# Five big, thirteen middle and fourteen small expert places instead of six big and twenty-six middle

## The chip, the cores and the metric

One core of one Trainium2 chip runs the whole program. The metric is the device time of one execution in microseconds, the median of several runs. A profiled execution gives the trace: each engine's instructions, the DMA transfers and the granted clock of TensorE.

## The reference

The program computes three transformer layers for one sequence of 256 tokens of 1024 channels. The first layer has a differential and a neighbourhood attention and then a mixture of experts; the other two are a retention and sparse-attention mixer, a gated recurrence, and two dense feed-forward layers. The change is in the mixture of experts alone, which in the reference comes down to this:

```python
logits = (hf @ w_router + b_router).astype(jnp.float32)     # 256 tokens, 32 experts
top_val, top_idx = lax.top_k(logits, TOP_K)                 # TOP_K = 4
gates = jax.nn.softmax(top_val, axis=-1)
...
hh = xb @ w1[e] + b1[e]                                     # 1024 -> 2048
return swiglu_clamped(hh) @ w2[e] + b2[e]                   # 1024 -> 1024
...
out = jnp.einsum('tk,tkd->td', gates.astype(y.dtype), y)
```

`swiglu_clamped` takes the even columns of `hh` as gate and the odd ones as line. Each token goes to four of the 32 experts, so an expert has 32 tokens on the mean, and some have many more. All weights are float32: an expert has 8 MB of `w1` and 4 MB of `w2`.

## The kernel before

The experts are worked off in 32 places, in a loop over `p` in `experts()` (L890). A place has a fixed number of slots for tokens, in units of `CAP` = 64: `UNITS` gives two units (128 slots) to places 0, 5, 10, 15, 20 and 25 and one unit (64 slots) to the other 26. Expert 0 has place 0, because its weights can be loaded before the routing is known. The other experts are sorted by their number of tokens on the chip (`places()`, L621), and the largest get the big places, through a table of ranks (`order` in `prep`). A token beyond the slots of its place would be computed by `overflow()` (L1032), a branch over all experts that is taken only if there is such a token.

The weights of a place come as 12 tiles of [128, 2048] float32 (1 MB): eight of `w1`, one for each chunk `dc` of 128 input channels, and four of `w2`. `load_e` (L782) issues them on SP's queue into a ring of 13 slots, always in the order of their use (`tile_e`, L771); a load waits until the products of the tile that has its slot are done. Loads and products are in the order in which the code writes them, since TensorE and SP are scheduled by hand in this stage.

For a place of 64 slots the tokens are the stationary operand, [128, 64], and the weights stream through in pieces of 512 columns. Two products, for two pieces of columns, go to partitions 0 to 63 and 64 to 127 of the output, as two column tiles of the array. A float32 product shows in the trace as two instructions, so a tile of `w1` is eight instructions (`w1`, L914; all products are recorded at L89 by the helper `mm`). For a place of 128 slots the full width of the array is taken, and every half tile of weights is first split in two exact parts by ScalarE and VectorE (`split_e`, L789), for three products in a faster format (`product`, L1023).

Column tiles of 32 occur in the kernel already: `ada_rows` and `steps_ada` multiply a vector with `w_ada` at the start of the program, four pieces of 512 columns at once on four groups of 32 partitions (tiles `ps_s<-w,cs` in the trace; the prediction calls them the adaptive rows).

One turn of the loop over `p` goes: evacuate the first products of `p` (`evac`, L797, its two ScalarE copies are recorded at L803); the first `w1` tile of place `p + 1`; transposes and activation of `p` (`swiglu`, L806); two more `w1` tiles of `p + 1`; the one-hot of the slots (`one_hot`, L832); the four `w2` tiles of `p`; the other five `w1` tiles of `p + 1`, with steps between them that scatter the rows of `p` to their tokens (`scatter`, L849) or gather the tokens of a later group of places (`gather`, L723). A group takes consecutive places up to four units; a gather is four products of each half of the tokens with a one-hot of up to 256 columns.

After the last place, `first_ffn` (L871) loads eight tiles of the next layer on the same queue (L62), adds the gated sum to the residual, and the mixer of the second block begins.

Of the kernel before, what the change touches and what calls it, by code (L numbers as in the profile page):

```python
# [21 lines left out]
UNITS = [2 if p in (0, 5, 10, 15, 20, 25) else 1 for p in range(NE)]  # L22
# [7 lines left out]
class Block:  # L30
# [34 lines left out]
    def prepare(self, src, pool, tags, w=None, lo_on=None):  # L65
        """takes the next product's first weight tile and splits it ahead of the products."""
        nc = self.nc
        w = w or self.load_w(src, 2048)
        parts = [pool.tile([128, 2, 1024], F32R, name=t) for t in tags]
        for q in range(2):  # L70
            wq = w[:, q * 1024:q * 1024 + 1024]
            hi, lo = (t[:, q] for t in parts)
            nc.scalar.copy(hi, wq)
            (lo_on or nc.vector).tensor_tensor(lo, wq, hi.bitcast(F32), op=OP.subtract)
            self.halves.append((hi, lo))
        self.ahead.insert(0, w)
# [88 lines left out]
    def spread(self):  # L165
        """1 / rms by token along the free axis, on every partition."""
# [34 lines left out]
    def proj_tm(self, src, hh, hl, n=512):  # L201
        """token-major product of a [128, 8, n] weight group: psum [128, 2, n]."""
# [5 lines left out]
    def steps_tm(self, p, src, hh, hl, n=512):  # L208
        """the same in four steps."""
# [14 lines left out]
    def proj_out(self, src, nk, mh, ml, by=1):  # L224
        """token-major product of nk [128, 1024] weight rows: two psum tiles [128, 2, 512], as in down()."""
# [29 lines left out]
    def softmax_unit(self, P, s, bias, rs):  # L255
        """P = exp(s + bias - max), row sums in rs."""
# [50 lines left out]
    def steps_ada(self, p, c0, n):  # L307
        """a step for each weight tile."""
# [11 lines left out]
    def ada_cols(self, rows):  # L320
        """[128, quadrant, 4] columns of the four pieces."""
# [5 lines left out]
    def gate_parts(self, rows, prow):  # L327
        """(gate + bias) * g_post in the rows, still in their parts."""
# [3 lines left out]
    def gate_rows(self, dst, rows):  # L332
        """dst [128, 1024] = the rows on every partition."""
# [195 lines left out]
    def transpose_probs(self, P):  # L529
        """P [128 q, 2 qt, 256 k] -> [128 k, 2 kc, 256 q] in sbuf."""  # L530
# [9 lines left out]
    def add_gated(self, srcs, g):  # L540
        """x += g * rms(src)"""
# [12 lines left out]

    def route(self):
        """the four experts of a token, their gates and the places of the tokens in the experts."""
# [54 lines left out]
        # experts by their number of tokens; expert 0 keeps the first place  # L611
# [9 lines left out]
    def places(self):  # L621
        """experts in the order of their places, and what belongs to them."""
# [54 lines left out]
    def biases(self):  # L677
        """the first biases at the places of their experts, [128 f, gate or line, (f block, half), place]; two steps."""
# [20 lines left out]
    def late(self):  # L699
        """steps: the second biases, and whether a token is beyond its expert's slots."""  # L700
# [22 lines left out]
    def gather(self, ps):  # L723
        """transposed, modulated tokens of the places ps, [128, 8, slots] each, and the steps that make them."""
        nc = self.nc
        n = sum(UNITS[p] for p in ps) * CAP
# [7 lines left out]
        for p in ps:  # L734
            w = UNITS[p] * CAP
            at[p] = slice(k, k + w)
            k += w
            if UNITS[p] == 2:
# [7 lines left out]
        def onehot():  # L746
            for p in ps:
                for tt in range(2):
                    self.last_oh = nc.vector.tensor_scalar(oh[:, tt, at[p]], self.slots[:, CAP:CAP + UNITS[p] * CAP],
# [21 lines left out]
    def tile_e(self):  # L771
        """the place of the weight tile that comes next for the products."""
# [16 lines left out]
    def split_e(self, w):  # L789
        """a half of a weight tile in two exact parts."""  # L790
# [6 lines left out]
    def evac(self, hid, hs, late):  # L797
        """products [128, 2, 512], even and odd columns apart."""
        copy = self.nc.vector.tensor_copy if late else self.nc.scalar.copy
        hp = hid.rearrange("p a (j two) -> p two a j", two=2)  # L800
# [5 lines left out]
    def swiglu(self, hs, b1):  # L806
        """act [128 f, blocks of f, slots]; b1 [128, 2, blocks]."""
        nc, moe = self.nc, self.moe
        k = b1.shape[2]
        pg, pu = self.bank("s"), self.bank("s")  # L810
        for j in range(4):
            nc.tensor.transpose(pg[:, j * 128:j * 128 + 128], hs[:, 0, j * 128:j * 128 + 128], self.ident)
        for j in range(4):
            nc.tensor.transpose(pu[:, j * 128:j * 128 + 128], hs[:, 1, j * 128:j * 128 + 128], self.ident)
        view = lambda t: t.rearrange("p (j s) -> p j s", j=k)

        def biased(ps, u, name):
            t = moe.tile([128, 512], F32, name=name)
            nc.vector.tensor_tensor(view(t), view(ps), b1[:, u, :, None].to_broadcast([128, k, 512 // k]), op=OP.add)
            return t  # L820
# [3 lines left out]
        act = moe.tile([128, 512], F32, name="act", bufs=2)  # L824
# [7 lines left out]
    def one_hot(self, p):  # L832
        """tokens of the slots [slot, token], and the gates of the slots."""
        nc, moe = self.nc, self.moe
        s = self.slots[:, 64:192] if UNITS[p] == 2 else self.slots[:, 0:128]
        wt = self.bank("t")
        for tt in range(2):
            go = moe.tile([128, 128], F32, name="go", bufs=2)
            nc.vector.tensor_scalar(go, s, self.pos[:, tt, p:p + 1], self.G[:, tt, p:p + 1], op0=OP.is_equal,
# [9 lines left out]
    def scatter(self, ys, ot, gs, first):  # L849
        """steps that add the gated rows to their tokens; ys: one [(half, slot), 512], or two halves [slot, 512]."""  # L850
# [39 lines left out]
    def experts(self):  # L890
# [3 lines left out]
        for p in range(1, NE):  # L894
            if len(groups) <= 2 or sum(UNITS[q] for q in groups[-1]) + UNITS[p] > 4:
                groups.append([])
# [17 lines left out]
        def w1(p, dc, w=None):  # L914
# [5 lines left out]
            if p not in hids:  # L920
                hids[p] = [self.acc() for _ in range(UNITS[p])]
            w = w or self.load_e("w1", ids[p], dc)
            for m in range(2):
                if UNITS[p] == 2:
                    self.product(hids[p][m], Xs[p][0][:, dc], Xs[p][1][:, dc], w[:, m * 1024:m * 1024 + 1024], dc)
            if UNITS[p] == 1:
# [45 lines left out]
        for p in range(NE):  # L972
            hs = self.ap.tile([128, 2, 2, 512], F32, name="hs", tag="hh")
            hs = [self.evac(h, hs[:, m], m) for m, h in enumerate(hids[p])]
# [5 lines left out]
            two = UNITS[p] == 2  # L980
            b1 = self.b1[:, :, :, p]
            acts = [self.swiglu(h, b1[:, :, m::2] if two else b1) for m, h in enumerate(hs)]
# [11 lines left out]
            for c2 in range(4):  # L994
                w = self.load_e("w2", ids[p], c2) if p else w20[c2]
                for j in range(2):
                    c = 2 * c2 + j
                    wj = w[:, j * 1024:j * 1024 + 1024]
                    if two:
                        k = slice((c % 4) * 128, (c % 4) * 128 + 128)  # L1000
                        self.product(ys, parts[c // 4][0][:, k], parts[c // 4][1][:, k], wj, c)
                    else:
# [20 lines left out]
    def product(self, outs, xh, xl, w, k):  # L1023
        """outs [128 slots] += x @ half a weight tile, in three exact products."""
# [7 lines left out]
    def overflow(self):  # L1032
        """the tokens beyond the slots: every expert over all tokens, gated by what is left."""
# [56 lines left out]

    def even_mixer(self):
# [16 lines left out]
        # compressed keys and values  # L1108
# [140 lines left out]
        # retention  # L1249
# [64 lines left out]
    def odd_mixer(self):  # L1314
# [19 lines left out]
        for h in range(8):  # L1334
# [36 lines left out]
            while L <= 128:  # L1371
# [16 lines left out]
                # the second blocks of qp and the first of ks, T - L further on  # L1388
# [97 lines left out]
    def finish(self, ys):  # L1486
        """rms(x + ys) * final_g; ys: a psum tile for each half of the tokens."""
# [66 lines left out]
def prep(i, cap=CAP):  # L1554
    """Lays the inputs out; the tables depend on shapes alone."""
# [34 lines left out]
    c0[:, 672:704] = np.array(UNITS) * cap  # L1590
    order = [p for p in range(1, NE) if UNITS[p] == 2] + [p for p in range(1, NE) if UNITS[p] == 1]
# [106 lines left out]
```

## Time and profile before

| What | us |
|---|---|
| median of 3 runs (lowest, highest) | 1940.81 (1940.6, 1941.16) |
| the profiled execution: first to last instruction (its span; no other time of it is listed) | 1948.8 |
| TensorE busy in it | 1863.1 (96%) |
| VectorE, ScalarE busy | 1029.9 (53%), 728.9 (37%) |
| weights of the experts: 384 loads of 1024 KB, first and last issue | 142.3, 1206.5 |

The times of the trace count from the first instruction of the profiled execution. A matmul's end is modelled and overlaps the start of the next, so a busy TensorE may still be waiting for the next operand; the starts are the surer reading. A load has an issue time, on SP's queue, and a landing.

### The profile page before, as it was taken

The numbers are of one execution on the slowest core, as the hardware profiler recorded it, in microseconds if no ns is written. First come the engines' busy times: TensorE is split into PE (matmuls) and PEld (weight loads), VectorE is DVE, ScalarE is ACT, GpSimd is POOL, SyncE is SP. The second block draws the span as 40 slices with busy tenths as digits, with TensorE's granted clock in tenths as the row PEclk, the third lists the DMA queues.
The fourth block names the chain that finished last, engine by engine and source line by source line (L and its number), as shares of the span: only waits on it lengthen the run. The fifth ranks groups of instructions, "written<-read, shape, count | busy, mean of one in ns | idle before, by whom it ended". The sixth has DMA issues, their size and how long they took to land. (4 is left out here: it accounts for less than half of the span.)

```text
span 1948.8 us, 27834 instructions
## 1 busy us (share of the span) xinstructions
PE 1863.1 (96%) x10815; PEld 1195.1 (61%) x10815; DVE 1029.9 (53%) x1795; ACT 728.9 (37%) x1250; POOL 53.1 (3%) x101
## 2 busy tenths in 40 slices
PE   6999999999999999989999999799999999999998
PEld 4776653454353354445345433487899988779997
DVE  3555653463463265346347232457666666856555
ACT  3445531342251142234134101345544444545443
POOL 0000000000000000000000000200000000110000
PEclk8999899999999999999999999899999999999999
DMA  9874689999989999998999999642455544344540
GB/s 395 308 257 191 264 337 422 420 352 385 422 344 403 421 398 370 392 420 323 416 421 357 390 415 421 241 152 87 152 196 193 190 171 140 118 154 169 180 170 22
DMA packets 79992, 564.28 MB, mean 290 GB/s; under 512 B 8960, under 2 KB 9120, under 8 KB 13296
## 3 DMA queue, kind: packets, MB, share of 16 engines
q1 hardware_dynamic: 78800, 557.58, 72.7%
q0 software_dynamic: 1056, 4.87, 0.7%
q8 instruction: 87, 1.43, 0.3%
q14 instruction: 49, 0.40, 0.1%
HBM read 561.37 MB, written 1.05 MB: 289 GB/s over the span
## 5 line engine op out<-in xcount | busy, mean ns | idle before, releaser
L89 PE MATMUL acc<-w,X 128*64 128x512 f32 x1664 | 392.0, 601 | 0.2 <-ACT hs L803 0.2
L85 DVE TENSOR_TENSOR wlo<-w,whi 128x1024 fp32r<-128x1024 f32 (+1 forms) x232 | 281.0, 1214 | 185.0 <-ACT whi L84 184.7
L84 ACT CAST whi<-w 128x1024 fp32r<-128x1024 f32 (+1 forms) x232 | 240.9, 1044 | 315.6 <-PE acc L89 131.4
L89 PEld LDWEIGHTS acc<-w,X 128*64 128x64 f32 x1664 | 106.7, 136 | 203.7 <-issue 187.6
L794 DVE TENSOR_TENSOR elo<-w,ehi 128x1024 fp32r<-128x1024 f32 x144 | 174.5, 1221 | 35.1 <-ACT ehi L793 34.4
L89 PE MATMUL ps_s<-w,act 128*64 128x512 f32 x832 | 185.6, 599 | 3.0 <-issue 3.0
L793 ACT CAST ehi<-w 128x1024 fp32r<-128x1024 f32 x144 | 149.6, 1049 | 69.8 <-PE acc L89 52.4
L867 DVE TENSOR_TENSOR macc<-macc,ps_t 128x512 f32<-128x512 f32 x124 | 84.2, 687 | 142.8 <-PE ps_t L89 142.8
L856 DVE SCALAR_TENSOR_TENSOR yl<-ps_s,gslot,yh 128x512 fp32r<-128x512 f32 x38 | 28.0, 749 | 193.1 <-ACT yh L855 193.1
L89 PEld LDWEIGHTS ps_s<-w,act 128*64 128x64 f32 x832 | 58.0, 138 | 112.1 <-issue 103.1
L803 ACT COPY hs<-acc 128x512 f32<-128x512 f32 x64 | 34.4, 589 | 222.7 <-PE acc L89 222.7
L89 PE MATMUL acc<-hh,whi 128*128 128x256 f32 x368 | 109.5, 298 | 2.0 <-ACT whi L84 2.0
L89 PE MATMUL acc<-hl,whi 128*128 128x256 f32 x368 | 107.0, 291 | 0.0
L89 PE MATMUL acc<-hh,wlo 128*128 128x256 f32 x368 | 106.4, 289 | 0.5 <-DVE wlo L85 0.5
L89 PE MATMUL ps_s<-hh,whi 128*128 128x256 f32 x352 | 98.7, 280 | 0.0
L89 PE MATMUL ps_s<-hl,whi 128*128 128x256 f32 x352 | 98.3, 279 | 0.0
L89 PE MATMUL ps_s<-hh,wlo 128*128 128x256 f32 x352 | 98.2, 279 | 0.0
L855 ACT ACTIVATE yh<-ps_s,gslot 128x512 fp32r<-128x512 f32 x38 | 25.5, 687 | 187.0 <-PE ps_s L89 187.0
L89 PE MATMUL ps_t<-hh,whi 128*128 128x256 f32 x320 | 89.4, 279 | 0.0
L89 PE MATMUL ps_t<-hl,whi 128*128 128x256 f32 x320 | 89.3, 279 | 0.0
L89 PE MATMUL ps_t<-hh,wlo 128*128 128x256 f32 x320 | 89.3, 279 | 0.0
L89 PE MATMUL acc<-ehi,Xh 128*128 128x512 f32 x192 | 67.5, 434 | 14.5 <-ACT ehi L793 13.1
(423 smaller groups left out, 3383.5 us busy)
## 6 DMA issues: line engine op xcount, KB each, us to landing
w<-in_w_dram SPq DMA_DIRECT2D x384, 1024.0 KB, 9.9
w<-in_ffn_dram SPq DMA_DIRECT2D x66, 1024.0 KB, 4.7
w<-in_w_ada_dram SPq DMA_DIRECT2D x24, 1024.0 KB, 10.6
w<-in_w_in_dram SPq DMA_DIRECT2D x12, 1024.0 KB, 11.5
w<-in_even_cm_dram SPq DMA_DIRECT2D x8, 1024.0 KB, 7.0
w<-in_odd_qf_dram SPq DMA_DIRECT2D x8, 1024.0 KB, 5.3
w<-in_w_out_dram SPq DMA_DIRECT2D x4, 1024.0 KB, 8.2
w<-in_even_tm_dram SPq DMA_DIRECT2D x4, 1024.0 KB, 5.2
```

Source lines behind the costliest of these rows:

```text
L84: nc.scalar.copy(hi[:, :n], w)
L85: nc.vector.tensor_tensor(lo[:, :n], w, hi[:, :n].bitcast(F32), op=OP.subtract)
L89: self.nc.tensor.matmul(out, lhsT, rhs, start=start, stop=stop, skip_group_check=True)
L793: self.nc.scalar.copy(hi, w)
L794: self.nc.vector.tensor_tensor(lo, w, hi.bitcast(F32), op=OP.subtract)
L803: copy(hv[:, u], hp[:, u])
L855: nc.scalar.activation(yh[:, m], y, AF.Copy, scale=gs)
L856: nc.vector.scalar_tensor_tensor(yl[:, m], y, gs, yh[:, m].bitcast(F32), op0=OP.mult, op1=OP.subtract)
L867: nc.vector.tensor_tensor(self.macc[:, tt, m], self.macc[:, tt, m], q, op=OP.add)
```

## The change

A third class of place has 32 slots. Big places (128 slots) are 0, 4, 9, 14 and 19; places of 64 slots are 13 others; the remaining 14, among them 1, 5, 8, 10, 15, 20 and 24 to 31, have 32. The number of slots of each place stands in `SLOTS`, which takes the place of `UNITS` everywhere: in the ranks (the largest experts in the big places, the next in the middle ones, the rest in the small ones), in the limit beyond which a token overflows, and in the packing of groups (up to 256 slots, now 10 groups where there were 11).

In a small place the four pieces of 512 columns of a `w1` tile go to four groups of 32 partitions, as four column tiles of the array, and all land in one bank. The second products also use four column tiles: two for the two halves of the output columns, times two for even and odd chunks of the hidden channels, which are summed separately. The one-hot of the scatter repeats the 32 slots four times, so that the scatter's contraction adds the two sums. Evacuation, transposes and activation work on half as many columns. Loads, ring and order of the loop are as before.

```diff
-UNITS = [2 if p in (0, 5, 10, 15, 20, 25) else 1 for p in range(NE)]
+BIGS, FULLS = (0, 4, 9, 14, 19), (2, 3, 6, 7, 11, 12, 13, 16, 17, 18, 21, 22, 23)
+
+SLOTS = [128 if p in BIGS else 64 if p in FULLS else 32 for p in range(NE)]
...
-    def evac(self, hid, hs, late):
+    def evac(self, hid, hs, late, quarter):
...
+        if quarter:
+            hp = hid[:, 0].rearrange("p (j two) -> p two j", two=2)
+            for u in range(2):
+                copy(hs[:, u, :256], hp[:, u])
+            return hs
...
-    def swiglu(self, hs, b1):
+    def swiglu(self, hs, b1, quarter):
...
+        n = 256 if quarter else 512
+        if quarter:
+            both = self.bank("s")
+            pg, pu = both[:, :n], both[:, n:]
+            for u, ps in enumerate((pg, pu)):
+                to = ps.rearrange("p (t j x) -> p j t x", t=2, j=2)
+                for j in range(2):
+                    nc.tensor.transpose(to[:, j], hs[:, u, j * 128:j * 128 + 128], self.ident)
...
+        if w == 32:
+            s = self.slots[:, None, 0:32].to_broadcast([128, 4, 32])
...
-            if len(groups) <= 2 or sum(UNITS[q] for q in groups[-1]) + UNITS[p] > 4:
+            if len(groups) <= 2 or sum(SLOTS[q] for q in groups[-1]) + SLOTS[p] > 4 * CAP:
...
+            if SLOTS[p] == 32:
+                for t in range(2):
+                    for m in range(2):
+                        r, c = (2 * t + m) * 32, (2 * m + t) * 512
+                        self.mm(hids[p][0][r:r + 32, 0], Xs[p][:, dc], w[:, c:c + 512], start=(dc == 0), stop=(dc == 7))
...
+                    elif quarter:
+
+                        k = (c % 4) * 2 + c // 4
+                        for m in range(2):
+                            r = (2 * m + j) * 32
+                            self.mm(ys[0][r:r + 32], acts[0][:, k * 32:k * 32 + 32], wj[:, m * 512:m * 512 + 512],
+                                    start=(c2 == 0), stop=(c2 == 3))
...
-    c0[:, 672:704] = np.array(UNITS) * cap
-    order = [p for p in range(1, NE) if UNITS[p] == 2] + [p for p in range(1, NE) if UNITS[p] == 1]
+    c0[:, 672:704] = np.array(SLOTS) * cap // CAP
+    order = [p for w in (128, 64, 32) for p in range(1, NE) if SLOTS[p] == w]
```

## Rows read from the trace of the kernel before

**Rows 1.** The page: TensorE's total, then three strips of 40 slices.

```profile
PE 1863.1 (96%) x10815; PEld 1195.1 (61%) x10815; DVE 1029.9 (53%) x1795; ACT 728.9 (37%) x1250; POOL 53.1 (3%) x101
...
PEclk8999899999999999999999999899999999999999
DMA  9874689999989999998999999642455544344540
GB/s 395 308 257 191 264 337 422 420 352 385 422 344 403 421 398 370 392 420 323 416 421 357 390 415 421 241 152 87 152 196 193 190 171 140 118 154 169 180 170 22
```

**Rows 2.** Windows: stretch, its length, busy us by engine, granted clock, DMA share, GB/s.

```profile
142.00:280.00 138.00, 132.73 (x646) 87.84 (x646) 86.48 (x189) 71.09 (x136) 5.83 (x12) 0.95 0.68 258
280.00:306.00 26.00, 26.00 (x120) 8.77 (x118) 7.74 (x14) 3.16 (x7) 0.00 (x0) 1.00 0.96 390
280.00:1225.00 945.00, 912.01 (x3969) 411.16 (x3967) 424.40 (x669) 259.81 (x406) 0.59 (x1) 0.99 0.97 394
296.00:371.00 75.00, 73.76 (x329) 30.45 (x328) 27.22 (x50) 17.32 (x32) 0.00 (x0) 1.00 1.01 422
18.00:28.00 10.00, 8.34 (x67) 3.64 (x66) 1.27 (x3) 1.26 (x4) 0.00 (x0) 1.00 1.01 420
28.00:38.00 10.00, 6.37 (x27) 4.15 (x28) 6.58 (x15) 5.62 (x10) 0.00 (x0) 0.53 1.01 419
1240.00:1254.00 14.00, 6.38 (x25) 4.25 (x26) 11.04 (x14) 7.67 (x13) 8.92 (x9) 0.63 0.80 282
```

**Rows 3.** Who waited for whom, 280 to 1225: us, times, longest.

```profile
SPq L786 <- PE acc L89: 353.3, 169, 5.7
SPq L786 <- DVE elo L794: 190.5, 57, 5.7
SPq L786 <- PE ps_s L89: 125.2, 96, 2.3
...
PEld acc L89 <- DMA w<-in_w_dram: 13.5, 43, 0.4
```

**Rows 4.** ScalarE in order of time: the evacuations of first products; start, length.

```profile
241.22 1.06 ACT L803 COPY hs<-acc 128x512 f32<-128x512 f32 x2
...
951.31 1.07 ACT L803 COPY hs<-acc 128x512 f32<-128x512 f32 x2 [11.09 <-PE acc L89]
976.86 1.07 ACT L803 COPY hs<-acc 128x512 f32<-128x512 f32 x2 [11.09 <-PE acc L89]
1010.75 1.08 ACT L803 COPY hs<-acc 128x512 f32<-128x512 f32 x2
1048.54 1.07 ACT L803 COPY hs<-acc 128x512 f32<-128x512 f32 x2 [1.68 <-PE acc L89]
1084.27 1.07 ACT L803 COPY hs<-acc 128x512 f32<-128x512 f32 x2 [10.98 <-PE acc L89]
```

**Rows 5.** TensorE in order of time: products of 64 and of 32 columns.

```profile
957.89 7.09 PE L89 MATMUL ps_s<-w,act 128*64 128x512 f32 x32
...
21.63 3.64 PE L89 MATMUL ps_s<-w,cs 128*32 128x512 f32 x32
25.80 1.06 PE L89 MATMUL ps_s<-w,cs 128*32 128x512 f32 x8 [0.53 <-DMA w<-in_w_ada_dram]
28.29 1.71 PE L89 MATMUL ps_s<-w,cs 128*32 128x512 f32 x8 [1.43 <-DMA w<-in_w_ada_dram]
```

**Rows 6.** The loads of expert weights: issue (ns), first and last start, landing.

```profile
L786 SPq DMA_DIRECT2D w<-in_w_dram x384: 327/333/475, 142.3 to 1206.5; - x192
...
DMA to landing us min/median/max: 4.6/9.9/19.7
```

**Rows 7.** All engines in order of time at the end of the experts.

```profile
1225.76 1.07 ACT L803 COPY hs<-acc 128x512 f32<-128x512 f32 x2 [11.09 <-PE acc L89]
...
1230.75 8.42 PE L89 MATMUL ps_s<-w,act 128*64 128x512 f32 x32 [2.99 <-issue]
...
1253.87 0.40 PE L89 MATMUL acc<-hh,mh 128*128 128x256 f32 x1
```

More of the change, by code (lines that the diff above doesn't have):

```diff
@@ L725, in gather @@
         nc = self.nc
-        n = sum(UNITS[p] for p in ps) * CAP
+        n = sum(SLOTS[p] for p in ps)
         oh = self.moe.tile([128, 2, 4 * CAP], F32, name="oh")
@@ L734, in gather @@
         for p in ps:
-            w = UNITS[p] * CAP
+            w = SLOTS[p]
             at[p] = slice(k, k + w)
             k += w
-            if UNITS[p] == 2:
+            if w == 128:
                 Xh = self.moe.tile([128, ND, 2 * CAP], F32R, name="Xh")
@@ L748, in onehot @@
                 for tt in range(2):
-                    self.last_oh = nc.vector.tensor_scalar(oh[:, tt, at[p]], self.slots[:, CAP:CAP + UNITS[p] * CAP],
+                    self.last_oh = nc.vector.tensor_scalar(oh[:, tt, at[p]], self.slots[:, CAP:CAP + SLOTS[p]],
                                                            pos[:, tt, p:p + 1], self.rx[:, tt:tt + 1],
@@ L804, in evac @@
         return hs
-    def swiglu(self, hs, b1):
+    def swiglu(self, hs, b1, quarter):
         nc, moe = self.nc, self.moe
         k = b1.shape[2]
[L810 to L814, printed above, removed]
+        n = 256 if quarter else 512
[6 more added lines that the diff above has]
+                    nc.tensor.transpose(to[:, j], hs[:, u, j * 128:j * 128 + 128], self.ident)
+        else:
+            pg, pu = self.bank("s"), self.bank("s")
+            for j in range(4):
+                nc.tensor.transpose(pg[:, j * 128:j * 128 + 128], hs[:, 0, j * 128:j * 128 + 128], self.ident)
+            for j in range(4):
+                nc.tensor.transpose(pu[:, j * 128:j * 128 + 128], hs[:, 1, j * 128:j * 128 + 128], self.ident)
         view = lambda t: t.rearrange("p (j s) -> p j s", j=k)
         def biased(ps, u, name):
-            t = moe.tile([128, 512], F32, name=name)
-            nc.vector.tensor_tensor(view(t), view(ps), b1[:, u, :, None].to_broadcast([128, k, 512 // k]), op=OP.add)
+            t = moe.tile([128, 512], F32, name=name)[:, :n]
+            nc.vector.tensor_tensor(view(t), view(ps), b1[:, u, :, None].to_broadcast([128, k, n // k]), op=OP.add)
             return t
@@ L823, in swiglu @@
         nc.vector.tensor_scalar(gl, gl, 7.0, None, op0=OP.min)
-        act = moe.tile([128, 512], F32, name="act", bufs=2)
+        act = moe.tile([128, 512], F32, name="act", bufs=2)[:, :n]
         nc.scalar.activation(act, gl, AF.Sigmoid, scale=1.702)
@@ L834, in one_hot @@
         nc, moe = self.nc, self.moe
-        s = self.slots[:, 64:192] if UNITS[p] == 2 else self.slots[:, 0:128]
+        w = SLOTS[p]
+        s = self.slots[:, 64:192] if w == 128 else self.slots[:, 0:128]
+        if w == 32:
+            s = self.slots[:, None, 0:32].to_broadcast([128, 4, 32])
         wt = self.bank("t")
@@ L838, in one_hot @@
             go = moe.tile([128, 128], F32, name="go", bufs=2)
-            nc.vector.tensor_scalar(go, s, self.pos[:, tt, p:p + 1], self.G[:, tt, p:p + 1], op0=OP.is_equal,
+            nc.vector.tensor_scalar(go.rearrange("p (k s) -> p k s", k=4) if w == 32 else go, s, self.pos[:, tt, p:p + 1], self.G[:, tt, p:p + 1], op0=OP.is_equal,
                                     op1=OP.mult)
@@ L920, in w1 @@
             if p not in hids:
-                hids[p] = [self.acc() for _ in range(UNITS[p])]
+                hids[p] = [self.acc() for _ in range(2 if SLOTS[p] == 128 else 1)]
             w = w or self.load_e("w1", ids[p], dc)
             for m in range(2):
-                if UNITS[p] == 2:
+                if SLOTS[p] == 128:
                     self.product(hids[p][m], Xs[p][0][:, dc], Xs[p][1][:, dc], w[:, m * 1024:m * 1024 + 1024], dc)
-            if UNITS[p] == 1:
+            if SLOTS[p] == 32:
[3 more added lines that the diff above has]
+                        self.mm(hids[p][0][r:r + 32, 0], Xs[p][:, dc], w[:, c:c + 512], start=(dc == 0), stop=(dc == 7))
+            if SLOTS[p] == 64:
                 for n in range(2):
@@ L973, in experts @@
             hs = self.ap.tile([128, 2, 2, 512], F32, name="hs", tag="hh")
-            hs = [self.evac(h, hs[:, m], m) for m, h in enumerate(hids[p])]
+            two, quarter = SLOTS[p] == 128, SLOTS[p] == 32
+            hs = [self.evac(h, hs[:, m], m, quarter) for m, h in enumerate(hids[p])]
             if p + 1 < NE and group[p + 1] >= ng:
@@ L979, in experts @@
             w1(p + 1, 0)
-            two = UNITS[p] == 2
             b1 = self.b1[:, :, :, p]
-            acts = [self.swiglu(h, b1[:, :, m::2] if two else b1) for m, h in enumerate(hs)]
+            acts = [self.swiglu(h, b1[:, :, m::2] if two else b1, quarter) for m, h in enumerate(hs)]
             if two:
```

## The prediction

> **What bounds the kernel now.** I read the page first, for where the time lies, then windows over the expert stage, then who waits for whom there, then single engines in order of time. The strip of the page shows a long middle, slices 6 to 25, with TensorE and the DMA engines both near their tops [rows 1]. Two engines cannot both be the bound of one stage, so the next view is the stage itself. From 280 to 1225 us it moves 394 GB/s on the mean, while a stretch without a big place moves 422 with the DMA engines' share at 1.01 [rows 2]. That is the top of the queue. 945 us x 394 GB/s are 372 MB; at 422 they would take 882 us. So 63 us of the stage are DMA time not used.
>
> Who is late tells why. The loads on SP's queue wait 353 us for TensorE's first products, 190 for the split's low parts and 125 for the second products, that is, for a free slot of the ring; TensorE in turn waits 13.5 us in all for weights, never over 0.4 at once [rows 3]. So TensorE's work sets the order and the queue follows it, with 6% to spare.
>
> One engine in order of time gives the price of a place. The evacuation of a place's first products marks where one place ends: 25.55 us from one 64-slot place to the next (951.31 to 976.86); 33.9 where a gather is added, so a gather costs 8.3; then 37.8 and 35.7 around the big place 25, so a big place costs 12.2 in its first products and 10.2 in its second above a 64-slot one [rows 4]. The 31 steps from the first to the last sum up to 984.6 us (241.22 to 1225.76) [rows 4, 7]. A tile of 1.0486 MB takes 2.49 us at 421 GB/s, a place of 12 tiles 29.9. A 64-slot place is thus faster on TensorE than its weights can come, a big one slower, and the ring of 13 tiles evens this out until it is full: then the queue stands still.
>
> **The change, part by part.** *Quarter places.* Thirty-two instructions of 64 columns (four tiles of second weights) take 7.09 us; the kernel has the 32-column form already, in the adaptive rows: 32 instructions, also four tiles, in 3.64 [rows 5]. The four column tiles do run at once. A quarter place has 12 tiles, so it saves 3 x 3.45 = 10.35 us of TensorE, 6.9 in the first products and 3.45 in the second; 14 of them save 145. Its evacuation, transposes and activation halve, which I cost at nothing: they hide behind products. What the shorter cover lays bare (a swiglu chain behind two tiles of 0.9 us instead of 1.8) I bound by 0 and 2.5 us a place.
>
> *Big places.* One fewer: 22.4 us. *Gathers.* By the packing rule there are 10 groups instead of 11: 8.3 us. The one-hot with its repeated slots and the scatter have the sizes of before: nothing.
>
> TensorE's steps then sum up to 984.6 - 145 - 22 - 8 = 809 us, and the weights of the same 31 places need 31 x 29.9 = 927. The bound changes over: from here on it is the queue, and the sum must be made with bytes. All expert weights are 384 x 1.0486 = 402.7 MB. Until 280 us 138 x 258 = 35.6 MB had moved, some 1.6 of them other tensors [rows 2], so 368.7 MB are left. At 421 GB/s: 876 us, the last tile at 1156.
>
> To this come four corrections. Just after 280 the queue still loses 2 us (390 GB/s up to 306); place 1, now a quarter, frees its last five slots 4.3 us sooner, and its wider gather (256 columns for 192) gives 1.7 back [rows 2]: together nothing, within 3. Second, a full ring: a landing takes at least 4.6 us, two tiles' time [rows 6], so 11 landed tiles, 27 us, are the most TensorE can be behind without the queue standing still. By the step prices the lag, 27 at place 1, goes to 20 and 15 over places 2 and 3, then up by 16 at place 4 (big, with a gather): 4 over; its four second tiles take 17 us for 10 us of weights, another 4 or so over. Later big places start from a lag of 7 to 16 and come to 25 to 30 at most, at the limit. I take 8 us in all; the bounds are 0 and 20. Third, the tail. Now TensorE is behind at the end: the last loads are issued at 1206.5 [rows 6], the last products end at 1239.2 [rows 7]. Bound by the queue, it has nothing left but the last tile: 1 us, or 2 at the low clock, or up to 10 if it lags; I take 2. Place 31's swiglu (1225.8 to 1230.8) [rows 7] lies under the four tiles that come after it, 10 us. Fourth, the 14.7 us from the last expert product to the first of the next mixer (1239.2 to 1253.9) [rows 7] stay: its first weight tile, queued behind the experts', lands 2.5 us behind the last of them, about when its split is due. In that stretch the clock stood at 0.63 [rows 2]; I add 1 us.
>
> Last expert product: 1156 + 0 + 8 + 2 = 1166 against 1239.2, less 73; with the clock's 1 less 72. The profiled span of 1948.8 becomes 1877. The span is 8.0 us above the median of the timed runs; I take the gain off that, **1940.8 - 72 = 1869 us**.
>
> Against this speaks a clock. When the adaptive products ran at the queue's pace, each tile in a short burst with a wait before it, the granted clock over 28 to 38 us was 0.53, about the low level of 1.2 GHz, and a burst of eight that took 1.06 at the high level took 1.71 [rows 2, 5]. A TensorE that waits between quarter tiles will look the same. The Trainium skill (TensorE: Matmul & The Clock Gate, "HAM oscillation") says of this pattern that each burst then starts cold; the trace agrees, with the 0.53 beside 1.00. By that rule alone the run of eight quarter places at the end would double its TensorE time. By rows it is this: a quarter step is 25.55 - 10.35 = 15.2 us, up to 17.7 with what is laid bare, and doubled 30.4 to 35, hardly above the 29.9 of its weights; and where TensorE falls behind it no longer waits, and in the expert stage, where it hardly waits, the mean stood at 0.99 [rows 2]. So I keep it out of the sum.
>
> **The rivals.** *Low clock at the end.* Eight steps 0.5 to 3 us over their weights and a last place done at half pace: 4 to 25 us, say 12: 1881. For it: the 0.53; against: the ring's 27 us of cover.
>
> *The ring keeps filling.* If the four later big places each stop the queue as the five do now (63 us, 12.6 each), the sum has 50 instead of 8: 1911. For it: the 190 us that loads wait for the split; against: between them lie quarter places that empty the ring by 7.8 us each.
>
> *The four tiles don't overlap.* At two at a time TensorE's steps are 984.6 - 22 - 8 = 954: 31 less, 1910. Against it stand the 3.64 us.
>
> *The queue's pace sags.* Nothing here runs longer than 100 us at 422. At the stage's mean of 394 the 368.7 MB take 936 us: the gain falls to 12, 1929. The Trainium skill (DMA: Bandwidth & Descriptors, Specifications) lists about 358 GB/s as HBM's limit for one core; by it the weights would take an estimated 1030 us and the stage would end near 1320. The rows of 422 contradict it here.
>
> *Slower: the clock stays low.* If TensorE is at the low level for a share s of its 809 us, its steps take 809 (1 + s); they reach the 998 us of now (241.2 to 1239.2) at s = 0.23, and from there the kernel is slower. At a third it is +81, 2022 us: quarter places would have to pull their 64-slot neighbours down too (25.55 becomes 51). For it: the long dips are where TensorE waited. Against: the stage's mean is 0.99 with such waits in it [rows 2].
>
> That tokens fall beyond the slots, which would start the overflow branch, I exclude: counted from the reference's own routing, expert 0 has 33 tokens, the fifth largest of the others 48, the eighteenth 21.
>
> **How the numbers follow.** Forecast 0.58; low clock 0.18; ring 0.12; no overlap 0.04; sag 0.03; slower 0.05. The first two lie within 1855 to 1894: the low end is no full ring and no lag (8 + 2 + 1 and 3 less). With the milder half of the ring's case the range is 1855 to 1900 and leaves out under 0.2. 0.2% (3.9 us) is about what a measurement of this kernel tells from no change. Faster 0.94, same 0.01, slower 0.05.
>
> **What would show it.** Right: 421 or 422 GB/s from about 300 to 1160 us but for a dent at place 4; SP's waits for the ring's slots no longer bounding, and TensorE waiting for weights by far more than 13.5 us; quarter steps of 29.9 at the end; first mixer product near 1181. A first-product tile of a quarter place: eight instructions in 0.9 us. Wrong: gaps in GB/s at every big place (ring), quarter steps above 31 with the clock near 0.5 (low clock), eight instructions in 1.7 us at full clock (no overlap), 400 GB/s with TensorE waiting (sag).

## The result and the profile after

The changed kernel takes 1886.76 us (median of 4 runs, 1884.95 to 1891.45) against 1940.99: a ratio of 0.9704, 95% interval 0.9672 to 0.9736, 54 us less. The forecast was 1869, with a range of 1855 to 1900. The profiled execution spans 1885.4 us and took 1887.06; that of before spans 1948.8 and took 1950.19, 9 us over its median, and this is needed to read the differences below: between the traces lie 63.4 us, between the medians 54.2.

The page after, TensorE's total and the strips of 40 slices that answer to [rows 1]:

```profile
PE 1725.1 (91%) x10671; PEld 1108.1 (59%) x10671; DVE 975.0 (52%) x1756; ACT 687.0 (36%) x1210; POOL 53.0 (3%) x101
...
PEclk9999899999999999999989978899999999999999
DMA  9874789999999999999999999523555543345540
GB/s 394 317 257 175 288 328 418 392 391 420 421 421 420 422 418 420 421 412 420 422 421 421 421 421 421 211 90 115 196 181 190 197 174 118 108 146 201 185 151 23
```

The dents of before (352, 344, 323, 316 and so on in the GB/s strip) are gone but for 392 and 391 in slices 8 and 9 and 412 in slice 18, and the clock strip, which stood at 9 from slice 6 to slice 25, falls to 7 and 8 near the end of the expert stage. Windows, with the columns of [rows 2]:

```profile
280.00:1160.00 880.00, 779.86 (x3811) 327.14 (x3807) 367.22 (x620) 215.82 (x359) 0.59 (x1) 0.95 1.01 417
...
372.00:407.00 35.00, 32.31 (x177) 15.37 (x179) 24.60 (x40) 12.81 (x20) 0.00 (x0) 1.00 0.91 352
960.00:1160.00 200.00, 141.26 (x785) 32.84 (x777) 44.86 (x95) 18.42 (x47) 0.00 (x0) 0.85 1.01 421
```

417 GB/s stand over the stage, where [rows 2] had 394. The main dent is at 372 to 407 us, around the big place 4. Over the last eight small places TensorE is busy for 141 of 200 us and its granted clock is 0.85, and the queue runs at 421 all the same.

Who waited for whom, 280 to 1160, first SP's queue and then TensorE, as in [rows 3]:

```profile
SPq L788 <- DMA w<-in_w_dram: 408.6, 233, 2.7
SPq L788 <- PE acc L91: 111.9, 86, 4.4
SPq L788 <- DVE elo L796: 103.7, 36, 8.1
SPq L788 <- PE ps_s L91: 30.5, 38, 2.3
```

```profile
PEld acc L91 <- DMA w<-in_w_dram: 70.5, 55, 3.1
PEld ps_s L91 <- DMA w<-in_w_dram: 48.4, 23, 2.3
PE acc L91 <- DMA w<-in_w_dram: 34.8, 36, 2.2
...
PE ps_s L91 <- DMA w<-in_w_dram: 27.9, 27, 1.4
```

The direction has turned. SP waited 353 us for first products, now 112, and its longest wait is now for earlier loads of weights (409 us, before 13.4). TensorE's matmuls, which did not wait for weights, wait 63 us, and its weight loads 119 where they had 18.4 (13.5 of it on the first products). The time from issue to landing says the same: its median was 9.9 us [rows 6], now the queue always has work ahead of it.

```profile
L788 SPq DMA_DIRECT2D w<-in_w_dram x384: 327/333/540, 140.9 to 1149.4; - x192
...
DMA to landing us min/median/max: 4.7/19.7/20.6
```

One small place at work, second products on TensorE in order of time, and three evacuations on ScalarE:

```profile
1018.79 1.06 PE L91 MATMUL ps_s<-w,act 128*32 128x512 f32 x8 [1.15 <-DMA w<-in_w_dram]
1021.19 1.06 PE L91 MATMUL ps_s<-w,act 128*32 128x512 f32 x8 [1.33 <-DMA w<-in_w_dram]
1023.68 1.94 PE L91 MATMUL ps_s<-w,act 128*32 128x512 f32 x8 [1.42 <-DMA w<-in_w_dram]
1026.15 1.49 PE L91 MATMUL ps_s<-w,act 128*32 128x512 f32 x8 [0.54 <-DMA w<-in_w_dram]
```

```profile
1101.15 0.65 ACT L805 COPY hs<-acc 128x256 f32<-128x256 f32 x2 [12.76 <-PE acc L91]
1130.56 0.65 ACT L805 COPY hs<-acc 128x256 f32<-128x256 f32 x2 [11.67 <-PE acc L91]
1160.38 0.65 ACT L805 COPY hs<-acc 128x256 f32<-128x256 f32 x2 [10.82 <-PE acc L91]
```

Eight instructions, a whole tile, take 1.06 us, or 1.94 where the granted clock is 0.53 (window 1023.5 to 1026), close to the low level of 1.2 GHz. Either is less than the 2.49 us in which the next tile comes: the starts are 2.4 to 2.5 us apart all along. The step from place to place is 29.4 and 29.8 us, the time of 12 tiles. The end of the stage, TensorE and VectorE:

```profile
1169.19 1.06 PE L91 MATMUL ps_s<-w,act 128*32 128x512 f32 x8 [1.00 <-DMA w<-in_w_dram]
...
1181.05 2.74 DVE L553 SCALAR_TENSOR_TENSOR x<-agt,agr,x 128x512 f32<-128x512 f32 x4 [1.35 <-ACT whi L86]
...
1186.51 0.48 PE L152 MATMUL ps_t<-c,x 128*128 128x128 f32 x1 [11.54 <-issue]
...
1189.84 0.56 PE L91 MATMUL acc<-hh,mh 128*128 128x256 f32 x1
```

The last expert product ends at 1170.3, 69 us earlier than the 1239.2 of [rows 7]. But the first piece of the residual is there at about 1181.8 and the transposes that read it begin at 1186.5, with "issue" as the cause: nothing that the profile shows. From the last expert product to the first product of the mixer it is 19.6 us, where it was 14.7.

### The profile page after: what moved, and what is told of

It is laid out like the page before. It is cut to its first block, busy times and chain, and to the rows that moved or that the text cites. A ratio compares the mean times of both kernels' runs of the same rounds, so it can differ in the third digit from the quotient of the medians.

```text
span 1885.4 us, 27422 instructions
## 1 busy us (share of the span) xinstructions
PE 1725.1 (91%) x10671; PEld 1108.1 (59%) x10671; DVE 975.0 (52%) x1756; ACT 687.0 (36%) x1210; POOL 53.0 (3%) x101
## 5 line engine op out<-in xcount | busy, mean ns | idle before, releaser
L91 PE MATMUL acc<-w,X 128*32 128x512 f32 (+1 forms) x1728 | 323.5, 626 | 35.1 <-DMA w<-in_w_dram 34.8
L91 PE MATMUL ps_s<-w,act 128*32 128x512 f32 (+1 forms) x864 | 159.9, 658 | 33.0 <-DMA w<-in_w_dram 28.9
L91 PEld LDWEIGHTS acc<-w,X 128*32 128x32 f32 (+1 forms) x1728 | 72.0, 124 | 198.4 <-issue 125.4
L796 DVE TENSOR_TENSOR elo<-w,ehi 128x1024 fp32r<-128x1024 f32 x120 | 145.6, 1223 | 34.6 <-ACT ehi L795 34.3
L795 ACT CAST ehi<-w 128x1024 fp32r<-128x1024 f32 x120 | 124.7, 1049 | 65.2 <-PE acc L91 45.3
L91 PEld LDWEIGHTS ps_s<-w,act 128*32 128x32 f32 (+1 forms) x864 | 41.5, 127 | 130.0 <-issue 72.4
L874 ACT ACTIVATE yh<-ps_s,gslot 128x512 fp32r<-128x512 f32 x37 | 24.9, 686 | 190.2 <-PE ps_s L91 190.2
L91 PEld LDWEIGHTS ps_t<-yh,ot 64*128 64x128 f32 (+1 forms) x128 | 23.2, 191 | 103.1 <-issue 58.7
L91 PEld LDWEIGHTS acc<-hh,whi 128*128 128x128 f32 x368 | 70.0, 190 | 11.5 <-issue 7.1
```

Source lines behind the costliest of these rows:

```text
L91: self.nc.tensor.matmul(out, lhsT, rhs, start=start, stop=stop, skip_group_check=True)
L795: self.nc.scalar.copy(hi, w)
L796: self.nc.vector.tensor_tensor(lo, w, hi.bitcast(F32), op=OP.subtract)
L874: nc.scalar.activation(yh[:, m], y, AF.Copy, scale=gs)
```

## The experiments

**The kernel before, once more.** No edit.

> The kernel before, profiled once more. The trace of the changed kernel is 63.4 us shorter than that of before (1948.8 to 1885.4), the medians 54.2 (1940.99 to 1886.76), and the profiled execution of before took 1950.19 us in all. Theory: that execution was an odd one, so a second profile spans about 1939 to 1941 us, with the 9 us missing at one place that the two traces show (expert stage, or the start). Rival: profiling lengthens every execution of before by 8 to 9 us (its loads of weights or its code), then the second span is 1947 to 1950 again, and the true gain is 63.

Ten executions took 1940.12 to 1950.34 us, and the mean granted clock of each goes with its time:

```
us     1940.12 1940.95 1942.19 1944.43 1945.71 1948.84 1949.68 1949.92 1950.24 1950.34
clock  0.993   0.993   0.992   0.990   0.988   0.986   0.986   0.985   0.986   0.986
```

The new profile was again of a long one (1948.84 us, span 1947.3). So neither text has it: profiling does not lengthen every execution, the kernel itself spreads over 10 us, and the trace of before, at clock 0.985, lies at the long end of that. No trace of a short execution is there, so where the long ones lose their time was not seen. One place is suspect: from 142 to 280 us, ahead of most of the change, the clock is 0.95 in both traces of before, but 0.99 in four of the nine other traces here.

**All places but the big ones with 32 slots.**

```diff
-SLOTS = [128 if p in BIGS else 64 if p in FULLS else 32 for p in range(NE)]
+SLOTS = [128 if p in BIGS else 32 for p in range(NE)]
...
-    c0[:, 672:704] = np.array(SLOTS) * cap // CAP
+    c0[:, 672:704] = 999
```

> All 27 places that are not big get 32 slots; tokens beyond the slots are left out, and the limit that would start the overflow branch is lifted. TensorE's work falls by another 13 x 10.35 = 135 us, no load is changed. Theory that the loads are the bound: the last expert tile lands within 5 us of that of the changed kernel (1169.1), perhaps 6 us sooner where the ring was full at place 4; time 1880 to 1888 us, the granted clock lower still. Rival, TensorE (with its clock) still sets the end: 1780 to 1850 us.

Measured: 1875.68 us, ratio to before 0.9654 (0.9627 to 0.9680), some 4 us below the expected 1880 to 1888. Its window over the stage, and its end on TensorE:

```profile
280.00:1155.00 875.00, 701.83 (x3689) 270.29 (x3689) 346.83 (x613) 201.45 (x345) 0.59 (x1) 0.86 1.01 421
```

```profile
1162.51 1.07 PE L91 MATMUL ps_s<-w,act 128*32 128x512 f32 x8 [0.97 <-DMA w<-in_w_dram]
...
1175.38 0.45 PE L152 MATMUL ps_t<-c,x 128*128 128x128 f32 x1 [7.14 <-DVE x L553]
```

By the forecast's prices TensorE has 135 us less to do (more, since the packing now makes 8 groups of gathers instead of 10), and the last expert product comes 6.7 us earlier (1163.6), with 421 GB/s over the whole stage and no stop of the queue at place 4. The loads are the bound, and the clock, at 0.86 over the whole stage, takes nothing. The other 4 us of its gain are at the end: here the transposes follow the residual at once (1175.38, released by it).

**Sixteen loads fewer in the last eight places.**

```diff
-                w = self.load_e("w2", ids[p], c2) if p else w20[c2]
+                if p < 24 or c2 % 2 == 0:
+                    w = self.load_e("w2", ids[p], c2) if p else w20[c2]
```

> The last eight places load only two of their four tiles of second weights and use each twice (half of the second weights is left out); all products stay. 16 tiles x 2.49 = 39.9 us of loads are gone. Theory that the loads are the bound: the last expert product comes 35 to 40 us earlier, span near 1847. Rival, TensorE at the low clock is the bound of these places: under 10 us.

One run: 1846.79 us, 40 less than the changed kernel. A window over most of the stretch, and evacuations of its places:

```profile
960.00:1120.00 160.00, 124.84 (x757) 34.45 (x753) 44.84 (x95) 18.44 (x47) 0.00 (x0) 0.90 1.01 421
```

```profile
946.29 0.65 ACT L805 COPY hs<-acc 128x256 f32<-128x256 f32 x2 [7.36 <-PE acc L91]
...
970.52 0.65 ACT L805 COPY hs<-acc 128x256 f32<-128x256 f32 x2 [8.96 <-PE acc L91]
...
995.37 0.65 ACT L805 COPY hs<-acc 128x256 f32<-128x256 f32 x2 [10.81 <-PE acc L91]
...
1121.66 0.65 ACT L805 COPY hs<-acc 128x256 f32<-128x256 f32 x2 [11.46 <-PE acc L91]
```

Sixteen tiles at 2.49 us are 39.8 us. The seven steps from 946.29 to 1121.66 take 25.1 us on the mean, the time of ten tiles (24.9), where they took the time of twelve, while the queue keeps its 421 GB/s: TensorE had the room, and what is not loaded is saved in full. In the last place no tile was late, and its second products, two tiles used twice each, ran without a wait between them:

```profile
1125.56 3.64 PE L91 MATMUL ps_s<-w,act 128*32 128x512 f32 x32 [1.93 <-issue]
```

The last expert product ends at 1129.2, 41 us sooner.

**The new order and one big place fewer, without the 32-slot class.**

```diff
-SLOTS = [128 if p in BIGS else 64 if p in FULLS else 32 for p in range(NE)]
+SLOTS = [128 if p in BIGS else 64 for p in range(NE)]
```

> The new order with five big places, but all other 27 places at 64 slots: one part of the change alone. By the steps TensorE has 984.6 - 22 - 0 = 962 us (11 or 12 gathers), the end comes about 22 to 30 us earlier than before: 1911 to 1920 us, and TensorE is still the bound, with the ring full after big places. Rival, that the one big place less gives most of the gain and the 32-slot form little: 1885 to 1895 us.

Measured: 1926.98 us (1923.95 to 1932.82), ratio 0.9923 (0.9893 to 0.9954), some 15 us less than before and 7 more than the upper end of what was expected. Its window over the stage, and SP's two longest waits for TensorE and for loads there:

```profile
280.00:1200.00 920.00, 889.11 (x3898) 385.55 (x3894) 386.05 (x624) 228.91 (x370) 0.59 (x1) 0.99 0.98 399
```

```profile
SPq L788 <- PE acc L91: 257.2, 130, 5.7
SPq L788 <- DMA w<-in_w_dram: 159.7, 88, 2.5
```

This kernel has the limits of the one before: TensorE busy for 889 of 920 us at 0.99, the queue at 399 GB/s behind it, SP waiting 257 us for first products. Its last expert product ends at 1214.2. So of the 54 us, some 15 belong to the five big places in their new order, with one big place fewer, and some 40 to the 32-slot form with the gather group that it saves (by the packing rule this kernel still has 11 groups, as before). My price for the first part was 22.4 us, from 1239.2 to 1216.8; the trace has 25 between its own and that of before. But before's trace is one of a long execution (clock 0.985) and this one of a shorter (0.988). Like with like, the gain is 17.5 us between the longest (1950.3 to 1932.8) and 16 between the shortest (1940.1 to 1923.95), so some 5 us of my price were not saved; why was not seen.

**The big places two later.**

```diff
-BIGS, FULLS = (0, 4, 9, 14, 19), (2, 3, 6, 7, 11, 12, 13, 16, 17, 18, 21, 22, 23)
+BIGS, FULLS = (0, 6, 11, 16, 21), (2, 3, 8, 9, 13, 14, 15, 18, 19, 20, 23, 24, 25)
```

> The same numbers of places, with the big ones at 0, 6, 11, 16 and 21 instead of 0, 4, 9, 14 and 19, and a second small place ahead of the first of them. Theory: the queue stood still for about 6.5 us around place 4 (372 to 407 us) because the ring was full; with the lag of TensorE gone before the first big place that stall is gone and the last expert tile lands 5 to 8 us earlier, near 1162; time 1879 to 1883. Rival: the stall belongs to every first big place after place 0, then no change within 2 us.

Measured: 1882.52 us (1878.94 to 1884.79), ratio 0.9687 (0.9660 to 0.9714). The window that held the dent:

```profile
372.00:407.00 35.00, 31.37 (x130) 19.96 (x130) 24.27 (x33) 18.30 (x23) 0.00 (x0) 0.90 1.01 421
```

421 GB/s where the changed kernel had 352: with two more small places ahead of the first big one after place 0, the queue no longer stops in this window. The last expert product ends at 1162.0 for 1170.3. By the dent alone, 35 us x (421 - 352) / 421 = 5.7 us should come back; 8.3 did in these traces, 4 in the medians (1886.76 to 1882.52; the intervals of the two ratios overlap). Two more windows of this trace, and then one of the changed kernel, show why the 8.3 are not the dent:

```profile
142.00:280.00 138.00, 131.16 (x695) 84.66 (x697) 89.39 (x200) 72.41 (x141) 5.80 (x12) 0.99 0.74 275
...
860.00:900.00 40.00, 37.06 (x177) 24.43 (x179) 27.45 (x45) 19.47 (x28) 0.59 (x1) 0.91 0.94 371
```

```profile
142.00:280.00 138.00, 131.16 (x656) 86.67 (x658) 88.72 (x199) 72.83 (x142) 5.80 (x12) 0.95 0.70 262
```

Ahead of 280 us this execution moved 13 GB/s more, at a granted clock of 0.99 for 0.95: 1.8 MB, or 4 us of loads. That is not the order's doing, since the kernel with both edits below has the same order and moved 264 there, at 0.95. And a new stop stands at 860 to 900 us, in the time of the last big place, 21: 371 GB/s, 4.8 us. So the order moves a good part of the stop to a later place. It is worth some 4 us, as the medians have it: the kernel with both edits, with a start like that of the changed kernel and the same new stop (373 GB/s), ends its last expert product at 1165.9, 4.4 us sooner than the changed one. Behind the last product nothing has changed: the residual's first piece is there at about 1174.0, the transposes begin at 1178.7.

**The overflow branch left out.**

```diff
         self.prepare(None, self.ap, ("mh", "ml"), ahead[0], self.nc.gpsimd)
-        self.overflow()
```

> The changed kernel without the overflow branch (which no token takes here; it is left out). Theory of the late code load behind a jump: without the jump the code is loaded in sequence and the first transposes start within 0.5 us of the residual; about 5 us less, and some more for the branch's own waits (the first product of the next layer 8 to 10 us after the last expert product instead of 19.6). Rival, a late code load has nothing to do with the jump: the transposes still come 4 us after the residual.

One run: 1887.46 us. This leaves out the instructions that read the count of tokens beyond the slots and the jump that skips the loop for them. The residual's first two pieces on VectorE, and the first of the transposes on TensorE:

```profile
1184.16 1.41 DVE L553 SCALAR_TENSOR_TENSOR x<-agt,agr,x 128x512 f32<-128x512 f32 x2 [0.46 <-POOL agr L99]
```

```profile
1184.97 0.48 PE L152 MATMUL ps_t<-c,x 128*128 128x128 f32 x1 [6.45 <-DVE x L553]
```

Two pieces of 0.7 us stand in the first row, so the first of the two ends at 1184.86, and the transposes begin 0.1 us behind it. The 4.7 us of "issue" are gone, and the mixer's first product comes 15.0 us after the last expert product instead of 19.6. The total did not move, since in this execution the stage itself ended 4 us later (1174.3 for 1170.3). Some 2.4 us of that lie at 680 to 700 us, around the big place 14, where the queue moved 361 GB/s for 412; the rest stays open. What went with the branch is seen on the queues that bring the engines' code, in the view of DMA queues from 1170 to 1190 (packets, MB, share of 16 engines), first of the changed kernel and then without the branch:

```profile
q8 instruction: 4, 0.07, 1.4%
q14 instruction: 5, 0.04, 0.6%
```

```profile
q8 instruction: 1, 0.02, 0.3%
```

Three of q8's four loads and all of q14's are gone with the branch. I read this so: behind the jump the engines go on at another place of the program, which has to be loaded.

**Fewer loads queued behind the experts' weights.** The changed kernel puts eight tiles of the next layer on SP's queue behind the last expert tile; here three stay there, and GpSimd issues the other five after the gated sum's last scale.

```diff
-        ahead = [self.load_w(*t) for t in todo]
+        ahead = [self.load_w(*t) for t in todo[:3]]
...
         self.add_gated([self.macc[:, tt].rearrange("p a b -> p (a b)") for tt in range(2)], gt2)
+        with self.tc.issue_after(self.last_pool.ins):
+            for src, n in todo[3:]:
+                w = self.wp.tile([128, 2048], F32, name="w")
+                self.nc.gpsimd.dma_start(w[:, :n], src)
+                self.ahead.append(w)
```

> The changed kernel with only three of the eight tiles of the next layer queued right behind the experts' weights; the other five are issued by GpSimd after the gated sum's last scale. In the changed kernel TensorE starts the transposes of the next layer 4.7 us after the residual is ready (1181.8 to 1186.5), 1.2 us after a code load of 16 KB ended that began at 1184.1. Theory: that code load is late because the queue of weights keeps the DMA engines full; with the engines free from 1177 on it comes earlier and TensorE starts within 0.5 us of the residual: 4 to 5 us less at the first product of the next layer, some of it lost again where the five tiles come later. Rival: the load comes late because TensorE asks late (its own place in the code), then the 4.7 us stay.

Measured: 1877.81 us (1876.94 to 1879.98), ratio 0.9665 (0.9635 to 0.9695), 9 us less than the changed kernel. The same two places in its trace:

```profile
1178.43 1.42 DVE L553 SCALAR_TENSOR_TENSOR x<-agt,agr,x 128x512 f32<-128x512 f32 x2 [0.73 <-POOL agr L99]
```

```profile
1182.01 0.47 PE L152 MATMUL ps_t<-c,x 128*128 128x128 f32 x1 [8.44 <-DVE x L553]
```

The code does come sooner once the DMA engines are free: q8's two loads of 16 KB start 5.8 and 11.1 us after the last expert product, for 8.0 and 13.8 in the changed kernel. The wait of the transposes falls from 4.7 to 2.9 us (1179.14 to 1182.01), not to nothing, so the full queue is a part of it and the jump with its load another. In all six traces in which the transposes wait, this one and the two of the changed kernel among them, they begin 1.2 to 1.5 us after the second of these loads has ended. The kernel before, the one without the 32-slot class and the one with 27 small places have such a load too (in the last at 13.8 us again), but there the transposes begin before it has ended.

That is 1.8 of the 9 us. The residual itself came 0.9 us sooner behind the last product, the stage ended 1.7 us sooner in this trace (1168.6), and 4.8 came where I had not looked: from the mixer's first product to the end it is 690.8 us, for 695.6. With the five tiles issued elsewhere, the order of TensorE's products further on changed as well. The view of one tile has the 128 products for its compressed keys, with the instructions' shortest, median and longest time and the first and last start, of this kernel and then of the changed one:

```profile
L91 PE MATMUL ps_s<-kb,w x128: 217/218/238, 1205.1 to 1220.6; 64*64 64x30 f32 x128
```

```profile
L91 PE MATMUL ps_s<-kb,w x128: 217/218/239, 1205.6 to 1229.4; 64*64 64x30 f32 x128
```

They stand in one run here, and between products on the full array there. That this order is what saves the 4.8 us is not shown; the same stretch takes 690.5 us in the kernel with both edits below, which issues the five tiles likewise. So this experiment mixes two effects, and its 9 us say nothing on the code's load beyond the 1.8.

**Both, and the changed kernel once more.** The big places two later and the five loads issued by GpSimd, in one kernel; and the changed kernel with no edit.

> The later big places together with the late prefetch. If both gains are of their own, time is that of the late prefetch (1877.8) less the stall at the first big place (4 to 8 us): 1870 to 1875 us, the last expert tile near 1160, the transposes of the next layer at most 3 us after the residual. Rival: the sooner the weights end, the later the code, and one gain eats the other: 1877 to 1880.

> The changed kernel itself, on the same chip as the combination, for its spread. 1884 to 1892 us; the last expert tile again lands within 3 us of 1169, and the first transposes of the next layer again wait 4 to 5 us behind the residual. If the wait is gone here, it was an accident of one execution and not a property of this code.

Both together: 1874.23 us (1873.54 to 1875.71), ratio 0.9633 (0.9610 to 0.9656). The changed kernel on the same chip: 1888.83 us (1885.89 to 1891.38), ratio 0.9709 (0.9686 to 0.9733). Its last expert product ends at 1168.1; its queue stops at place 4 as before and once more around place 14 (362 GB/s from 680 to 700 us). The wait is there again:

```profile
1184.78 0.48 PE L152 MATMUL ps_t<-c,x 128*128 128x128 f32 x1 [11.69 <-issue]
```

The residual's first piece was there at 1180.0, 4.8 us ahead of it. The two edits give 14.6 us together; singly they gave 4 and 9. The weights did not end near 1160, as was expected, but at 1165.9. This is the shortest of the kernels here that load all weights. With 27 places of 32 slots, which does less, it was 1875.68.

## Why the prediction was right or wrong

*The bound changes over to the queue: right.* 417 GB/s over the stage, SP's waits turned into TensorE's, steps of a small place at 29.4 and 29.8 us for the 29.9 of its weights. The experiments show it from both sides: with at least 135 us less work for TensorE the stage ends 6.7 us sooner, with 40 us less loading it ends 41 sooner.

*The queue holds 421 GB/s: right.* 875 us at 421 in the kernel with 27 small places. The Trainium skill (DMA: Bandwidth & Descriptors, Specifications) has about 358 GB/s as one core's limit; one core alone held 421 here, and the measurement decides.

*Four column tiles overlap: right.* 1.06 us for a whole second tile, and 3.64 for the products of four in one run (the kernel with fewer loads), both as the 32-column form of [rows 5].

*A full ring at place 4, 8 us: right in the main.* The dent is 5.7 us by its bytes in 372 to 407; over the whole stage 417 GB/s for 421 are 8.4 us. Later big places come to the limit, as the forecast said, and in some executions over it: 2.8 us at place 14 in the repeated changed kernel, 0.4 there in the first. The rival of a ring that keeps filling had 50 us and does not stand.

*Last expert product: 1166 forecast, 1170.3 and 1168.1 measured.* 2 to 4 us of 73. The forecast left out what else moves in that time: from 280 to 1169.2 us the queues of code and of GpSimd moved 0.79 MB in the changed kernel, which at 421 GB/s is an estimated 1.9 us. The rest I do not assign.

*The tail: 2 us, measured 1.1* (the last product waits for its tile until 1169.2 and ends at 1170.3).

*The clock falls at the end but costs nothing: right, and the rival of the low clock falls.* It went to 0.85 over the small places, and bursts of 1.94 us stand beside those of 1.06. The Trainium skill (TensorE: Matmul & The Clock Gate, "HAM oscillation") says that bursts with waits between them start cold; the trace agrees in part, as two of the four bursts shown above, each behind a wait, took 1.06 us. But a cold tile is still done in 1.94 of the 2.49 us that the next one takes to come, and the stage that ran at 0.86 all through ended 6.7 us sooner than this one.

*"Fourth, the 14.7 us [...] stay": wrong, by 4.9 us.* They became 19.6. In the kernel before, TensorE was late at the end, and its transposes began at 1250.2, 0.2 us behind the residual's first piece. Now the last loads come late, and the next layer's tiles keep the DMA engines full just when the engines jump over the overflow branch and load new code. Without the branch the wait is gone; with five tiles taken from the queue it is 2.9 us; repeated, the changed kernel has 4.8 again. The kernel with 27 small places had a full queue, loads of code at the same 8.0 and 13.8 us and no wait, so neither the queue nor the late load makes it alone: its transposes did not wait for that load. That the code falls otherwise into its loads there is argued, not shown.

*"I take the gain off that" (the median): not sound, and by these two traces half of the miss.* The gain was worked out in an execution of 1950.19 us with its clock at 0.985, and taken off a median of 1940.8. Between the traces lie 63.4 us, between the medians 54.2: 9 us. Of the 18 us between 1869 and 1886.8 this is one half, and the end of the stage (4.3) and the wait behind it (4.9, less the 1 us that I had added for the clock) the other. I had seen the 8 us between span and median and took them for an offset that both kernels share; repeated executions show that they are spread, which goes with the clock (1940 us at 0.993, 1950 at 0.986).

My reading is that a kernel bound by TensorE pays for its clock and one bound by the queue does not, so that the gain against a long execution is larger than against a short one. For it: the kernel without the 32-slot class goes with its clock as well (1924 us at 0.990, 1933 at 0.984), while of the changed kernel's nine executions (1884.95 to 1891.45 us) the two longest had 0.958 and 0.964, the shortest 0.960. But it can be no full account. Like with like, the gain is 59 us between the longest executions (1950.2 to 1891.45) and 56 between the shortest (1940.6 to 1884.95), for a forecast of 72; so 13 to 16 us were not there whichever execution is taken, and beyond the 8 us of the stage's end and the wait they stay open. And ahead of 280 us the changed kernel seems to pay for its clock too, with 262 GB/s at 0.95 and 271 at 0.99 when repeated. The first experiment shows the spread; where before's long executions lose their time was not seen in a trace.

## What to carry to other kernels

When two engines of a stage both stand near their tops, work out the floor of each: here TensorE's 145 us saved were worth some 40, because the weights' bytes allow no more. Then look at what else needs the DMA engines when they are never idle: the engines' code behind a jump comes later, and may be waited for. Before a difference of two traces is put down to an edit, compare the stretch ahead of it: half of the 8.3 us between the traces of the later big places and of the changed kernel came from there. And compare a sum made in one execution with that execution, not with the median of others, and long executions with long ones, where the time varies with the clock.

## What the runs showed of the hardware

- The kernel before, one core alone, spreads over 10 us (1940.1 to 1950.3), and its mean granted clock with it (0.993 to 0.986).
- With the jump over a skipped branch the queues of code had three loads of 16 KB and five of 8 KB behind the stage that were not there without it. TensorE stood still behind the residual for 4.7 us while the queue of weights was full, 2.9 with fewer loads, 0.1 without the branch. But it stood only 0.2 in the kernel before and in the one with 27 small places, which have the jump too.
- 128 products on tiles of 64 x 64 took 15.4 us in one run, and 23.8 from first to last when they were mixed with products on the full array. The Trainium skill (TensorEngine Tiling (Array Packing), Key Properties) says that a change of tiling mode drains the array; the difference fits, but the second time holds those other products too, so the price of a switch is not measured.
- TensorE's clock at 0.86 for 875 us cost nothing, with 421 GB/s beside it.
- From 142 to 280 us, where the DMA engines were busy for 0.69 to 0.74 of the time, the clock of an execution goes with the bytes: with place 1 small, 261 to 266 GB/s in the traces at 0.95 or 0.96, 271 to 275 in those at 0.99.
